# Elementwise work of the mixers taken off GpSimd, the chunk inverse done for two streams at once, and another order of pages and first loads

## The chip, the cores and the metric

The kernel runs on one core of a Trainium2 chip. TensorE (PE) multiplies, VectorE (DVE) and ScalarE (ACT) do elementwise work and read PSUM, GpSimd (POOL) does elementwise work on SBUF, SyncE (SP) issues the DMAs. The metric is the time of one execution on the device in microseconds, as the median of several runs.

## The reference

Two layers over two streams of 256 tokens and 1024 channels, a context `ctx` and the input `x`. In each layer both streams are normalised and modulated by rows computed from `c` (`silu(c) @ w_ada + b_ada`), then pass a mixer, then 16 experts of which each takes its 32 best tokens. The mixer has three branches; the first, gated delta heads, runs in both directions and matters here:

```
q, k = l2_normalize(silu(conv(q))), l2_normalize(silu(conv(k)));  v = silu(conv(v))
decay = exp(gc[i] - gc[j]) for j <= i               # gc: running sum of the gates
m   = strict_lower((k*beta) @ k.T * decay);  a = m + I
u, w = solve(a, v*beta), solve(a, k*beta*exp(gc))   # unit triangular
per chunk:  v_new = u - w @ s
            o     = (q*exp(gc)) @ s + (q @ k.T * decay) @ v_new
            s     = s*exp(g_last) + (k*exp(g_last - gc)).T @ v_new
o = rmsnorm(o_forward + o_backward) * gdn_norm_w * silu(z)
```

The state at the end of `ctx` is the start for `x`. The second branch is a gated token mixing over chunks of 128, the third a pooling; the three are gated, projected and added (`merge`). In layer 1 the context runs only for its states. Experts: `silu(x@w_gate) * (x@w_up) @ w_down`, all in fp32.

## The kernel before

**A recorded program and a planner.** `Net.record` and what it calls write no instructions. Each call on an engine makes an `Op` with its operands (`Prog.record`); `Prog.order` then simulates the engines with a cost for every op (`Prog.cost`), hands out SBUF and PSUM as it goes, and gives each engine a fixed order, which `Prog.emit` issues. An `Eng` with several names (`ad`, `av`, `any`, `vg`) leaves the choice of the engine to the planner. All instructions are issued from one line, so every row of the profile says L623 and tiles are named only `page` (SBUF) and `bank` (PSUM).

**Memory.** SBUF is 25 pages of 2048 fp32 elements per partition. `place` looks for a hole: for short-lived tiles from page 0 up, first in pages of the same size class, then in empty pages, then anywhere; only expert weights take pages in the order in which these became empty. `limits` cap the live tiles of a kind: `wa=5` modulation weights, `w=4` projection weights, `we=18` expert weights. A tile given to a DMA must be free before the DMA can be issued, and SP issues in order.

**PE's two queues.** `order` keeps ready 32x32 matmuls (`op.tile`) apart from the rest, takes them when the wide ones leave room, and leaves a group of them at the latest after twelve (`quad`) if wide ones are ready.

**The order of the work.** `ada_in(0)` loads 16 modulation tiles of 512 KB in two halves, with one pair of matmuls each. `ctx` is loaded ahead of them, `x` after the seventh. Then per layer: norms, `start`, and `gdn`. `gdn` goes over four pairs of heads j. For each it records, for the context and then for `x`, the scan (`heads_scan`) and, behind it, that stream's solve for the next pair (`heads_solve`), and takes pieces of other work (projections, the other branches in `side`) in between, `FILL` many. `pump` mixes in modulation blocks (`ada`), one load step at a time.

**The solve and the inverse.** `heads_solve` builds the decay (`E`, `Eb`), the products with keys and queries (`MT`, `attn`, `qt`) and calls `inverse`: for one stream, 8 matrices of 128x128 (two chunks, two directions, two heads). It inverts the 32x32 diagonal blocks in four levels, each one group of 32 small matmuls, a mask on DVE in two halves, a second group of 32, an add and a transpose; then joins blocks to 64 and to 128 in four more groups. GpSimd does the elementwise steps that carry `G` in the code, and some of those with `vg` and `any`.

**After the heads** come the rest of `side` (gates and branch projections), `merge`, the routing and the experts, whose weights (201 MB a layer) stream in 1 MB tiles.

Of the kernel before, what the change touches and what calls it, by code (L numbers as in the profile page):

```python
# [102 lines left out]
def _layouts(inp):  # L103
# [14 lines left out]
    o["gnw"] = f(g["gdn_norm_w"])  # L118
# [103 lines left out]
class Op:  # L222
    __slots__ = ("i", "eng", "fn", "a", "k", "tiles", "deps", "succ", "nd", "cost", "ready", "start", "end", "on", "prio", "gate", "inst", "win", "tile", "fill")
# [34 lines left out]
class Prog:  # L258
    def __init__(s, nc, pool, banks, limits):
# [6 lines left out]
        s.any = Eng(s, ("act", "dve", "pool"))  # L266
        s.av, s.vg = Eng(s, ("act", "dve")), Eng(s, ("dve", "pool"))
# [13 lines left out]
    def record(s, eng, fn, a, k):  # L281
# [43 lines left out]
        if (not op.deps or eng[0] == "dma") and lim not in ("w", "wa", "we"):  # L325
            op.win = min(op.win, 400)
        if lim in ("w", "wa", "we"):
            op.win = 10 ** 9
        op.tile, op.fill = False, 1.0
# [6 lines left out]
    def cost(s, op, acc):  # L336
# [16 lines left out]
        if op.eng[0] == "pe":  # L353
            if op.fn == "transpose":
                return {"pe": n * 2 / 2.4 + 2}
            m = acc[0][0].shape[0]
            op.fill = min(m, 128) * acc[1][0].shape[0] / 16384
# [3 lines left out]
            c = max(n, m) / 1.2 * 2 + 4  # L361
            return {"pe": c if m > 64 else c * (0.6 if m > 32 else 0.25) + 20 if n < 128 else c * (0.5 if m > 32 else 0.25) + 14}
# [10 lines left out]
    def order(s):  # L373
# [29 lines left out]
        def place(t, spare):  # L403
# [6 lines left out]
            if t.lim == "we":  # L410
                order = sorted(order, key=lambda i: freed[i])
            for step in range(3):
                if step == 1 and sum(g is None for g in pages) <= spare:
                    continue
                for i in order:
                    g = pages[i]
                    if (g is None) != (step == 1) or (g is not None and (g.dt != dt or (step == 0 and g.cls != cls))):
# [39 lines left out]
        def give(t, addr):  # L457
# [9 lines left out]
            if j > 0 and hs[j - 1][1] == a:  # L467
                hs[j - 1:j + 1] = [(hs[j - 1][0], hs[j][1])]
            if hs[0] == (0, PAGE):
                pages[page.i] = None  # L470
                turn[0] += 1
                freed[page.i] = turn[0]
# [11 lines left out]
        recent, group = [], [None, 0]  # L484
# [21 lines left out]
        while left:  # L506
# [6 lines left out]
            while ev and ev[0][0] <= now:  # L513
                _, i, kind = heapq.heappop(ev)
                op = ops[i] if i >= 0 else None
                if kind == 0:
                    for e in op.eng:
                        heapq.heappush(ready["tile" if op.tile else e], (op.prio, op.i))
# [5 lines left out]
            for e in engines:  # L524
# [3 lines left out]
                if e == "pe":  # L528
# [3 lines left out]
                    if ready["tile"]:  # L532
# [5 lines left out]
                        if ready[e] and (x < ready[e][0] and not much or ops[x[1]].a[0].tile is group[0] and group[1] % s.limits["quad"]):  # L538
                            queues.reverse()
                aside, tries = [], 0  # L540
                while queues:
# [26 lines left out]
                    if e == "pe":  # L568
                        if not span[3]:
                            c *= 2  # L570
                        if group[0] is not None and not op.tile:
                            c += 80.0
                        group[1] = group[1] + 1 if op.tile and op.a[0].tile is group[0] else 1
                        group[0] = op.a[0].tile if op.tile else None
                        span[1] += c * op.fill
                        span[2] += c
                        if not op.tile:
# [48 lines left out]
XAT = 6  # L626
# [4 lines left out]
POOLW = (0, 6)  # L631
# [5 lines left out]
FILL = (3, 1, 1)  # L637
ROOM = dict(w=0, wa=0)
EVERY = (0.7, 1.0)
NY = 3  # L640
# [12 lines left out]
class Net:  # L653
# [43 lines left out]
    def run(s):  # L697
        tc, t = s.tc, s.t
        limits = dict(w=4, hi=5, wa=5, we=18, fill=0.94, window=800, spare=0, clock=4096 / 1.2, share=0.5, quad=12, room=ROOM)
# [9 lines left out]
    def record(s):  # L709
# [26 lines left out]
        nc.sync.dma_start(s.xin[0], s.rows[0].rearrange("(t p) d -> p t d", p=128))  # L736
        s.small = {}
        for n, sh in (("n1", [128, 2, 8]), ("conv", [128, 2, 24, 5]), ("psc", [128, 2, 4]), ("wr", [128, 2, 8, 16]),
                      ("alog", [128, 2, 16]), ("dtb", [128, 2, 16]), ("gnw", [128, 2, 128])):
# [8 lines left out]
        for n, _ in enumerate(s.ada_in(0)):  # L748
            if n == EAT:
                s.mark = len(p.ops)  # L750
            if n == XAT:
                nc.sync.dma_start(s.xin[1], s.rows[1].rearrange("(t p) d -> p t d", p=128))
        p.bias = LATE
        nc.sync.dma_start(s.cst[:, C_CUM:C_LEN], t["cst"][:, C_CUM:C_LEN])
        for n in ("conv", "psc", "wr"):
            nc.sync.dma_start(s.small[n], t[n])
        for n, w in (("alog", 16), ("dtb", 16), ("gnw", 128)):
# [59 lines left out]
    def ada(s, l, parts):  # L817

        nc, t = s.nc, s.t
        for g, halves in parts:  # L820
            ps = s.bank("ada")
            js = [j for a in halves for j in (2 * a, 2 * a + 1)]
            for kt in range(8):
                ws = {}
                for a in halves:
# [1021 lines left out]
```

## Time and profile before

| | |
|---|---|
| median of 3 runs | 2430.93 us (2430.82 to 2431.25) |
| profiled execution | 2433.34 us, its span 2431.6 us |
| busy: PE, DVE, ACT, POOL | 2118.4, 1172.9, 647.9, 370.6 us |
| DMA | 603.11 MB, mean 248 GB/s |
| chain that ended last | PE 45%, DMA 36%, DVE 12%, issue 3%, POOL 2%, ACT 1% |

Busy time is the union of an engine's instructions. PEld is the loading of weights, which overlaps PE. A matmul in fp32 shows as two records. The chain of waits is followed back from an end: at each step to what released it; "issue" is time in which nothing that the profile shows was waited for.

### The profile page before, as it was taken

What the parts mean: (1) busy time and instruction counts of PE and PEld (TensorE: products, weight loads), DVE (VectorE), ACT (ScalarE), POOL (GpSimd) and SP (SyncE); (2) the same over time, 40 slices, a digit from 0 to 9 for tenths busy, and PEclk for the clock granted to TensorE, in tenths of its full rate; (3) what the DMA queues carried; (4) which work ended last, traced back from release to release, by engine and by line L of the source; (5) the groups of instructions that cost most, each with busy time, mean ns of one, the idle gap of its engine ahead of it and who ended that gap; (6) DMA issues with size and microseconds to landing.
All of it is one profiled execution on the core that took longest, in us unless ns stands there. A gap on an engine that the chain in (4) does not pass through costs nothing.

```text
span 2431.6 us, 50016 instructions
## 1 busy us (share of the span) xinstructions
PE 2118.4 (87%) x21357; PEld 1351.6 (56%) x21357; DVE 1172.9 (48%) x2712; ACT 647.9 (27%) x1329; POOL 370.6 (15%) x334
## 2 busy tenths in 40 slices
PE   8999999999999999878787899999899977676665
PEld 4777867787779842222222477777789931111211
DVE  4978776854326831212121797788765531010102
ACT  4534343323224520000000454344434420000000
POOL 0233332510000410000000212232330010000000
PEclk9999999999999999999999999999899988888888
DMA  8432333323346689999999634333236879999997
GB/s 291 146 101 82 117 90 99 99 102 101 118 162 203 214 320 421 421 421 421 421 421 421 243 113 152 128 118 122 69 101 217 317 315 421 421 421 421 422 421 307
DMA packets 153910, 603.11 MB, mean 248 GB/s; under 512 B 13820, under 2 KB 60092, under 8 KB 104536
## 3 DMA queue, kind: packets, MB, share of 16 engines
q1 hardware_dynamic: 153688, 599.93, 64.9%
q8 instruction: 167, 2.74, 0.4%
q14 instruction: 55, 0.45, 0.1%
HBM read 597.58 MB, written 2.29 MB: 247 GB/s over the span
## 4 chain that ended last, share of the span: by engine, by line
PE 45%; DMA 36%; DVE 12%; issue 3%; POOL 2%; ACT 1%; SPq 0%; DVEq 0%; ACTq 0%; POOLq 0%
PE bank L623 45%; DMA page<-in_w_up_dram 22%; DVE page L623 12%; DMA page<-in_w_down_dram 12%; POOL page L623 2%; ACT page L623 1%; DMA page<-in_w_gate_dram 0%; DMA page<-in_n_dram 0%; DMA page<-in_b_ada_dram 0%; DMA page<-rows 0%; SPq L623 0%; DMA page<-in_w_ada_dram 0%; DVEq L1843 0%; DVEq L623 0%; POOLq L623 0%
## 5 line engine op out<-in xcount | busy, mean ns | idle before, releaser
L623 PE MATMUL bank<-page,page 32*32 32x32 f32 (+8 forms) x18473 | 2074.4, 335 | 299.6 <-DVE page L623 107.3
L623 PEld LDWEIGHTS bank<-page,page 128*128 128x128 f32 (+5 forms) x18473 | 1300.2, 144 | 1048.4 <-issue 381.3
L623 POOL TENSOR_TENSOR page<-page,page 128x512 f32<-128x512 f32 (+4 forms) x277 | 313.5, 1146 | 1444.1 <-DVE page L623 1050.3
L623 ACT ACTIVATE page<-page 128x1024 fp32r<-128x1024 f32 (+8 forms) x462 | 326.5, 721 | 534.2 <-PE bank L623 273.6
L623 ACT ACTIVATE page<-bank 128x512 f32<-128x512 f32 (+5 forms) x341 | 164.9, 501 | 1106.9 <-PE bank L623 1012.1
L623 DVE TENSOR_TENSOR page<-page,page 128x1024 fp32r<-128x1024 f32 (+6 forms) x389 | 338.5, 888 | 118.9 <-ACT page L623 102.0
L623 DVE TENSOR_TENSOR page<-page,bank 128x256 f32<-128x256 f32 (+2 forms) x184 | 101.4, 558 | 575.9 <-ACT page L623 269.1
L623 DVE TENSOR_TENSOR page<-bank,page 128x128 f32<-128x128 f32 (+4 forms) x350 | 154.5, 460 | 287.2 <-PE bank L623 282.6
L623 ACT ACTIVATE page<-page,page 128x128 f32<-128x128 f32 (+2 forms) x319 | 119.9, 435 | 50.2 <-POOL page L623 31.2
L623 DVE COPY page<-bank 32x128 f32<-32x128 f32 (+7 forms) x175 | 71.4, 408 | 60.9 <-PE bank L623 58.9
L623 DVE SCALAR_TENSOR_TENSOR page<-page,page,page 128x508 f32<-128x508 f32 (+3 forms) x128 | 94.5, 757 | 1.2
L623 DVE SCALAR_TENSOR_TENSOR page<-page,page 128x508 f32<-128x508 f32 (+5 forms) x115 | 75.9, 665 | 14.1 <-DMA page<-in_n_dram 11.7
L623 PE MATMUL bank<-page 32*32 32x32 f32 (+1 forms) x2884 | 76.2, 204 | 2.8 <-DVE page L623 2.4
L623 PEld LDWEIGHTS bank<-page 32*32 32x32 f32 (+1 forms) x2884 | 59.2, 114 | 20.0 <-issue 8.5
L623 POOL MEMSET page<- 128x1024 f32 (+2 forms) x13 | 7.6, 630 | 398.6 <-DMA page<-in_w_up_dram 389.7
L623 DVE TENSOR_SCALAR page<-page 128x4 f32<-128x4 f32 (+7 forms) x215 | 52.6, 258 | 26.2 <-ACT page L623 19.2
L623 DVE STREAM_TRANSPOSE page<-page 32x32 f32<-32x32 f32 (+1 forms) x208 | 57.8, 288 | 4.2
L623 DVE SCALAR_TENSOR_TENSOR page<-page,bank 128x512 f32<-128x512 f32 x48 | 32.7, 684 | 55.9 <-PE bank L623 54.7
L623 ACT ACTIVATE page<-bank,page 128x128 f32<-128x128 f32 (+2 forms) x81 | 36.7, 483 | 78.5 <-PE bank L623 60.0
L623 DVE TENSOR_TENSOR page<-page 128x4 f32<-128x4 f32 (+3 forms) x252 | 50.5, 209 | 4.1
L623 POOL TENSOR_TENSOR page<-page 128x512 f32<-128x512 f32 x22 | 30.9, 1406 | 138.7 <-DVE page L623 96.1
L623 DVE TENSOR_SCALAR page<-page,page 128x128 f32<-128x128 f32 (+3 forms) x125 | 47.4, 416 | 5.2 <-ACT page L623 4.8
(25 smaller groups left out, 235.5 us busy)
## 6 DMA issues: line engine op xcount, KB each, us to landing
page<-in_w_gate_dram SPq DMA_DIRECT2D x128, 1024.0 KB, 19.8
page<-in_w_up_dram SPq DMA_DIRECT2D x128, 1024.0 KB, 19.8
page<-in_w_down_dram SPq DMA_DIRECT2D x128, 1024.0 KB, 19.8
page<-in_w_in_dram SPq DMA_DIRECT2D x136, 512.0 KB, 3.6
page<-in_w_ada_dram SPq DMA_DIRECT2D x96, 512.0 KB, 4.6
page<-rows SPq DMA_DIRECT2D x88, 256.0 KB, 5.0
page<-in_w_br_a_dram SPq DMA_DIRECT2D x24, 512.0 KB, 4.7
page<-in_w_out_dram SPq DMA_DIRECT2D x24, 512.0 KB, 4.6
```

The source lines that it names most:

```text
L623: op.inst = getattr(eng[op.on], fn)(*a, **k)
```

## The change

All elementwise work of the mixers goes to DVE or ACT; GpSimd keeps memsets, the routing's steps and the last norm. `gdn_norm_w` is no longer multiplied into `zs` but is the scale of ACT's last copy (per partition there). The square in `heads_out` becomes four ACT instructions with a running sum, the two products after it one DVE instruction per head and chunk, the state's decay a `scale` on ACT or DVE. `heads_solve` takes both streams, and `inverse` handles 16 matrices in each instruction; `gdn` records it once per j, behind the context's scan. `NY` falls from 3 to 2 buffers, each twice as large. The planner gets other PE costs, puts all matmuls with 64 or fewer rows or columns in the second queue, and stays there while any is ready. Short-lived tiles take pages in the order of their last release, and with more than 8 pages empty also empty ones. The first 16 modulation tiles may all be live (`wi=16`), `ctx` is loaded after the fourth and `x` after the eighth; `ada` loads and multiplies two blocks a step. Core of the diff:

```diff
-            m = acc[0][0].shape[0]
-            op.tile = m <= 32 and acc[1][0].shape[0] <= 32
+            m, k = acc[0][0].shape[0], acc[1][0].shape[0]
+            op.tile = m <= 32 and k <= 32
+            op.part = m <= 64 or k <= 64
             if acc[2][0].dtype == F32R and n >= 256:
-                return {"pe": n / 2.4 + 2}
+                return {"pe": n / 2.4 + 13.5}
...
+            if op.tile:
+                return {"pe": 9.0}
...
-            if t.lim == "we":
+            empty = sum(g is None for g in pages)
+            if not up:
                 order = sorted(order, key=lambda i: freed[i])
-            for step in range(3):
+            for step in range(0 if up or empty <= ROOMY else -1, 3):
...
-    if ready[e] and (x < ready[e][0] and not much or ops[x[1]].a[0].tile is group[0] and group[1] % s.limits["quad"]):
+    if ready[e] and (x < ready[e][0] and not much or group[2]):
         queues.reverse()
...
-XAT = 6
+ROOMY = 8
+XAT = (3, 7)
-POOLW = (0, 6)
-FILL = (3, 1, 1)
+FILL = (6, 1, 2)
-NY = 3
+NY = 2
-        limits = dict(w=4, hi=5, wa=5, we=18, ..., quad=12, room=ROOM)
+        limits = dict(w=4, hi=5, wa=5, wi=16, we=18, ..., room=ROOM)
...
-            if n == XAT:
-                nc.sync.dma_start(s.xin[1], s.rows[1]...)
+            if n in XAT:
+                k = XAT.index(n)
+                nc.sync.dma_start(s.xin[k], s.rows[k]...)
...
-                w = s.p.tile([128, 2, 512], F32, name="wada", lim="wa")
+                w = s.p.tile([128, 2, 512], F32, name="wada", lim="wi" if l == 0 else "wa")
...
-        s.tt(lo, w, hi.bitcast(F32), ALU.subtract, s.p.vg if s.wn > POOLW[s.l] else nc.gpsimd)
+        s.tt(lo, w, hi.bitcast(F32), ALU.subtract)
...
-                if j < 3:
-                    sol[m.k] = s.heads_solve(m, j + 1, qkv[j + 1][m.k], slot(m, j + 1))
+                if j < 3 and m is ms[0]:
+                    sol = s.heads_solve(ms, j + 1, qkv[j + 1], Y[(j + 1) % NY], X[(j + 1) % NY])
                     take(FILL[2])
...
+    def heads_solve(s, ms, j, qkv, Y, XF):
+        MT = [s.p.tile([128, 8, 128], F32, name="MT") for d in range(2)]
+        part = {m.k: s.products(m, j, qkv[m.k], [a[:, 4 * z:4 * z + 4, :] for a in MT]) for z, m in enumerate(ms)}
+        s.inverse(MT, Y, XF)
...
-            s.tt(E, R[0], s.nb[:, :, None, :].to_broadcast(B4), ALU.add, G)
+            s.tt(E, R[0], s.nb[:, :, None, :].to_broadcast(B4), ALU.add)
...
         for lv in range(1, 5):
-            Pn = s.p.tile(C5, F32, name="Pn")
-            for i in range(2):
-                s.tt(Pn[:, i], pp[:, i], s.nm[:, lv, :, None, :].to_broadcast([128, 2, 2, 32]), ALU.mult)
+            Pn = s.p.tile(C4, F32, name="Pn")
+            s.tt(Pn, pp, s.nm[:, lv, :, None, :].to_broadcast(C4), ALU.mult)
```

## Rows read from the trace of the kernel before

**Rows 1.** Stretch, us; busy us (instructions) per engine; PEclk, DMA share, GB/s.

```profile
60.00:520.00 460.00, 434.93 (x7016) 349.27 (x7014) 352.77 (x937) 186.70 (x439) 149.92 (x137) 0.99 0.33 104
520.00:870.00 350.00, 345.93 (x2063) 286.96 (x2061) 175.80 (x272) 122.69 (x191) 44.58 (x31) 1.00 0.48 163
600.00:700.00 100.00, 100.00 (x435) 75.10 (x434) 35.56 (x39) 26.05 (x33) 4.49 (x3) 1.00 0.34 117
950.00:1000.00 50.00, 42.02 (x170) 13.13 (x166) 12.88 (x19) 1.19 (x2) 0.00 (x0) 1.00 1.01 421
1345.00:1820.00 475.00, 439.92 (x7078) 342.88 (x7075) 376.85 (x999) 214.69 (x493) 136.12 (x125) 0.97 0.39 126
128.38:128.95 0.57, 0.57 (x65) 0.57 (x64) 0.57 (x4) 0.57 (x3) 0.00 (x0) 1.00 1.04 423
```

**Rows 2.** Chain of waits, 60 to 520, then 1345 to 1820 us; shares.

```profile
by line: PE bank L623 58.1%; DVE page L623 26.2%; issue 7.8%; POOL page L623 4.7%; ACT page L623 1.6%; DMA page<-rows 1.4%; SPq L623 0.2%; DVEq L623 0.0%; POOLq L623 0.0%; ACTq L623 0.0%
...
by line: PE bank L623 59.8%; DVE page L623 27.7%; issue 6.4%; POOL page L623 3.1%; ACT page L623 3.0%; DVEq L623 0.0%; ACTq L623 0.0%; POOLq L623 0.0%
```

**Rows 3.** PE's weight loads in time order: start, us, form, count, idle before.

```profile
130.12 0.51 PEld L623 LDWEIGHTS bank<-page,page 32*32 32x32 f32 x25 [0.36 <-DVE page L623]
130.87 0.62 PEld L623 LDWEIGHTS bank<-page,page 32*32 32x32 f32 x26 [0.25 <-issue]
131.85 0.22 PEld L623 LDWEIGHTS bank<-page,page 32*32 32x32 f32 x16 [0.36 <-issue]
...
108.19 2.54 PEld L623 LDWEIGHTS bank<-page,page 32*32 32x32 f32 x74 [1.57 <-DVE page L623]
...
516.34 3.62 PEld L623 LDWEIGHTS bank<-page,page 32*32 32x32 f32 x58 [0.32 <-DVE page L623]
...
1435.02 2.14 PEld L623 LDWEIGHTS bank<-page,page 32*32 32x32 f32 x71 [0.37 <-DVE page L623]
...
1797.18 0.80 PEld L623 LDWEIGHTS bank<-page,page 32*32 32x32 f32 x35 [0.33 <-issue]
```

**Rows 4.** Waits in both head stretches: us, times, longest.

```profile
PEld bank L623 <- issue: 33.2, 64, 2.7
...
PEld bank L623 <- issue: 47.0, 97, 3.1
...
DVE page L623 <- ACT page L623: 16.3, 29, 2.0
```

**Rows 5.** DVE by operands, 60 to 520 us: ns min/median/max.

```profile
L623 DVE SCALAR_TENSOR_TENSOR page<-bank,page,page x36: 340/343/351, 203.4 to 475.9; 128x128 f32<-128x128 f32 x36
...
L623 DVE SCALAR_TENSOR_TENSOR page<-page,page,page x60: 704/746/1772, 90.5 to 383.7; 128x508 f32<-128x508 f32 x30, 128x510 f32<-128x510 f32 x30
...
L623 DVE COPY page<-page x48: 172/217/1453, 134.3 to 515.7; 32x128 f32<-32x128 f32 x48
```

**Rows 6.** DVE by form, 60:520, 1345:1820, 1820:1947: busy, mean ns, idle before.

```profile
L623 DVE COPY page<-page 32x128 f32<-32x128 f32 x48 | 13.4, 294 | 0.6
L623 DVE SCALAR_TENSOR_TENSOR page<-page,page,page 128x510 f32<-128x510 f32 x30 | 25.6, 855 | 0.4
L623 DVE STREAM_TRANSPOSE page<-page 128x256 f32<-128x256 f32 x40 | 17.6, 440 | 0.6
L623 DVE TENSOR_TENSOR page<-bank,page 128x128 f32<-128x128 f32 x64 | 15.7, 282 | 17.6 <-PE bank L623 17.6
L623 DVE TENSOR_TENSOR page<-page,bank 128x256 f32<-128x256 f32 x44 | 17.9, 418 | 39.3 <-PE bank L623 39.2
...
L623 DVE COPY page<-page 32x128 f32<-32x128 f32 x58 | 20.6, 376 | 0.6
...
L623 DVE TENSOR_TENSOR page<-page,page 128x512 f32<-128x512 f32 x5 | 3.5, 693 | 0.2
```

**Rows 7.** GpSimd by form, 60 to 520 us: busy, mean ns, idle before.

```profile
L623 POOL TENSOR_TENSOR page<-page,page 128x512 f32<-128x512 f32 x75 | 101.3, 1365 | 230.7 <-DVE page L623 160.3 <-PE bank L623 42.5 <-DMA page<-rows 14.9
```

**Rows 8.** Busy time from 0 to 40 us, columns as in rows 1.

```profile
0.00:40.00 40.00, 29.25 (x127) 11.19 (x129) 13.26 (x43) 14.65 (x23) 4.23 (x11) 0.96 0.88 322
```

More of the change, by code (lines that the diff above doesn't have):

```diff
@@ L222 @@
 class Op:
-    __slots__ = ("i", "eng", "fn", "a", "k", "tiles", "deps", "succ", "nd", "cost", "ready", "start", "end", "on", "prio", "gate", "inst", "win", "tile", "fill")
+    __slots__ = ("i", "eng", "fn", "a", "k", "tiles", "deps", "succ", "nd", "cost", "ready", "start", "end", "on", "prio", "gate", "inst", "win", "tile", "part", "fill")
 class Eng:
@@ L409, in place @@
             order = range(PAGES - 1, -1, -1) if up else range(PAGES)
-            if t.lim == "we":
+            empty = sum(g is None for g in pages)
+            if not up:
                 order = sorted(order, key=lambda i: freed[i])
-            for step in range(3):
-                if step == 1 and sum(g is None for g in pages) <= spare:
+            for step in range(0 if up or empty <= ROOMY else -1, 3):
+                if step == 1 and empty <= spare:
                     continue
@@ L517, in order @@
                     for e in op.eng:
-                        heapq.heappush(ready["tile" if op.tile else e], (op.prio, op.i))
+                        heapq.heappush(ready["tile" if op.part else e], (op.prio, op.i))
                 elif kind == 1:
@@ L570, in order @@
                             c *= 2
[L571 to L574, printed above, removed]
+                        if group[2] and not op.part:
+                            c += 225.0
+                        elif op.part and not group[2]:
+                            c += 95.0
+                        group[2] = op.part
                         span[1] += c * op.fill
                         span[2] += c
-                        if not op.tile:
+                        if not op.part:
                             recent.append((now, c * op.fill))
@@ L1433, in inverse @@
+        yc = s.p.tile([128, 8, 32], F32, name="Y32")
+        V.tensor_copy(yc, yy)
         for a, b in ((0, 1), (2, 3)):
-            V.tensor_copy(Y[Q[a], :, 0, :, 32 * b:32 * b + 32], yy[Q[a]])
-            V.tensor_copy(Y[Q[b], :, 1, :, 32 * a:32 * a + 32], yy[Q[b]])
-        for i in range(2):
-            for h in range(2):
-                V.transpose(XF[Q[1], i, h, 0:32], Y[Q[0], i, 0, h, 32:64])
-                V.transpose(XF[Q[2], i, h, 32:64], Y[Q[3], i, 1, h, 64:96])
+            s.p.av.copy(Y[Q[a], 0, :, 32 * b:32 * b + 32], yc[Q[a]])
+            s.p.av.copy(Y[Q[b], 1, :, 32 * a:32 * a + 32], yc[Q[b]])
```

225 lines of the change are left out of this document (112 added, 113 removed).

## The prediction

> **What bounds the kernel now.** First the stages. The table of busy time by stretch [rows 1] shows two kinds. While a layer's experts run, the DMA share is 1.01 at 421 GB/s and nothing else is full: that part is set by bytes, and the diff changes none of them. In between lie the mixers, about 0 to 880 us and 1345 to 1950 us, at 104 to 163 GB/s. In their second half (520 to 870 in layer 0) PE is busy 99%: a run of 128-wide matmuls with little to gain. In their first half, the delta-rule heads, PE is busy 434.93 of 460 us and 439.92 of 475 us, DVE 77% and 79%, POOL 33% and 29%. A microsecond saved in a mixer moves everything after it, as the expert stream starts when the mixer ends.
>
> Second, the chain of waits over the two head stretches [rows 2]. PE is 58.1% and 59.8% of it, DVE 26.2% and 27.7%, POOL 4.7% and 3.1%, issue 7.8% and 6.4%. So PE is not the bound alone: of 460 + 475 us, DVE holds 120.5 + 131.6 = 252 us and POOL 21.6 + 14.7 = 36 us. Three parts of the change touch these: who does the elementwise work, how many small-matmul groups there are, and how wide the DVE steps between them are.
>
> **Part 1, PE: fewer visits to the small tiles.** The inverse runs 32x32 matmuls; between them PE goes to 128-wide ones. The weight-load rows show what a round trip costs [rows 3]. From 130.12 to 130.87 us are 24 small loads and one wide one (x25): 0.75 us. 64 small matmuls take 0.57 us (128.38 to 128.95) [rows 1], so 24 take 0.21, and a wide one takes 100 us / 435 = 0.23 (600 to 700) [rows 1]. Left: 0.31 us. From 130.87 to 131.85, 24 small and two wide: 0.98 - 0.21 - 0.46 = 0.31 again. It shows as 0.25 to 0.37 us of idle ahead of each group, which the waits call "issue": 33.2 and 47.0 us [rows 4].
> Such groups number 97 in the first head stretch and 89 in the second; [rows 3] shows the first and the last of each. Eight inverses of ten groups would make 80: the old limit of twelve splits some. After, there are four paired inverses of ten groups a layer, and a rule that stays with the partial matmuls while any is ready: 40 + 40. 106 fewer at 0.31 is 33 us; 16 fewer groups of 64-wide matmuls at the same price make 5. PE and issue together hold 66% of the chain, so I take 25 of 38 us (ends 10 and 38).
>
> **Part 2, DVE freed of POOL.** The rows of DVE by operand [rows 5] give minimum, median and maximum. Where an operand lies in PSUM all are alike (340/343/351). Where all lie in SBUF the median is as fast, but the maximum is far off: copies of 32x128 172/217/1453, multiply-adds 704/746/1772. Against means of 294 and 376 ns for those copies and 855 for half of those multiply-adds [rows 6], layer 0 loses 48 x 0.077 + 30 x 0.109 = 7 us, layer 1 58 x 0.159 = 9 us, on forms that hold 39 and 21 us of busy time. Over all forms with SBUF alone I take some 20 us in each, 5.5% of DVE's work [rows 1], an estimate. With no POOL work in the mixers it goes. On the chain: 252 x 5.5% = 14 us (ends 0, and 45 if the blocked instructions all lie on it).
> [...]
>
> **Part 3, POOL's work moved.** What is on POOL's chain now is mostly 128x512 products at 1365 ns [rows 7]; DVE does one in 693 [rows 6]. 36 us on the chain become 18: minus 18 (ends 0, if DVE is queued, and 36). The load on DVE: POOL's 150 + 136 us at half is 143 us more (less, as squares and state scaling go to ACT, 41 to 45% busy, and one product is folded into a copy). Against it stand the 40 us above and the pairing, 74 us. So DVE ends a little above where it is, near 80%.
>
> **Part 4, the paired inverse on DVE.** Rows of the single inverse [rows 6]: a level takes two masks at 0.282, one add at 0.418, one transpose at 0.440, 1.42 us; four levels 5.7. With the nine masks and adds ahead, twelve block copies, eight 32x32 transposes and the last blocks, one inverse takes about 13.4 us by the nearest forms, a pair 26.8. Paired, a level is a mask of 0.69, an add of 0.69 and a transpose of about 0.72 (0.440 and 256 columns more at the 0.0011 by which 0.282 at 128 becomes 0.418 at 256): 2.1; four are 8.4, and the rest, counted in the same way with half the instructions at twice the width, 9.2. That is 17.6, 9.2 us less a pair, 37 a layer. Inverses are 107 of DVE's 353 us, so the chain's share is 252 x 30% x 34% = 26. I take 18, since PE no longer starts on the first half of a mask after 0.282 us but waits 0.69. Ends: 26 gained; 13 lost if all 32 levels wait the 0.4 us unhidden.
>
> **Part 5, the start.** By 40 us 322 GB/s x 40 = 12.9 MB have come, and PE is busy only 29 of the 40 us [rows 8]. Of the sixteen modulation tiles only five may live, so a load waits for the matmuls of one five ahead, and SP's queue with it. At 421 GB/s the bytes take 30.6 us. With 16 tiles nothing holds back the issues; ctx and x lie behind four and eight of them. At most 9 us; PE already has wide matmuls in between from 32 us, so I take 6 (ends 0 and 9).
>
> **Part 6, what I put at nothing.** Taking pages in the order of release removes waits on pages just let go; the nearest row is DVE's waits for ACT, 16.3 us in 29 [rows 4], few of which can be that: 0, up to 10 gained. It may cost room: Y and X64 grow from 3 x 1280 to 2 x 2560 elements, MT and one more set of attn and qt add some 3,000, two or three of 25 pages. Three megabytes of expert weights less fetched ahead are 7.5 us at 421 GB/s a layer: 0 to 15 lost. I take 0 because these tiles are dead when the experts are fetched. Two modulation blocks a step under the limit of five tiles have less lead, but PE goes to them half as often; no wait for them stands among PE's long ones, so 0, to 2 lost.
>
> **Sum.** 25 + 14 + 18 + 18 + 6 = 81. Span 2431.6 - 81 = 2350.6; the profiled execution took 2433.3, 1.7 more than its span and 2.4 more than the median, so 2350 against 2430.93. Its own range: 2305 to 2400.
>
> **Rivals.**
> *Only the visits pay* (0.18). DVE and POOL work is hidden behind PE, and the chain goes back to PE when they shrink. For it: PE is busy 93 to 95% of the head stretches. Against: 252 us of DVE on the chain. 25 + 6 = 31 saved: 2400.
> *DVE takes it back* (0.07). The 143 us land on a DVE that is already busy 77 and 79% [rows 1] and the savings of part 4 do not come on the chain. 143 - 74 - 45 = 24 more, which eats the visits: 2430.
> *One long chain* (0.16, slower). Paired, the solve is a single chain of 12 PE and DVE steps on which both streams' scans of the next head pair wait, where two inverses used to cover each other. Its length: a level is two PE rounds of about 1.45 us (DVE waits 39.2/44 = 0.9 now, for half the matmuls [rows 6]) and 2.1 of DVE, 5.0; four are 20; start 4.8 and the last blocks 8: 33 us, eight times 264. It decides when more than 81/8 = 10 us of each finds no wide matmul to cover it; at 13 us uncovered, 104 - 81 = 23 is lost: 2455. For it: layer 1 has fewer queries to project and already more PE idle, 35 against 25 us. Against: 97 groups a layer wait now, and the wide matmuls that cover them are not fewer.
> [...]
>
> **Chances.** Forecast 0.59, rivals 0.18, 0.07, 0.16. Under 0.2% (5 us) I cannot tell a change: faster 0.77, same 0.07, slower 0.16. The range to 2436 takes in all but the slower rival; 2300 leaves out the ends where all parts pay in full.
>
> **What would show it.** Right: about 40 small-tile groups a layer; copies of 32 rows near their median of 217, no maximum over 1 us; POOL empty between 90 and 870 us; DVE's share of the chain under 24%; the first modulation's bytes in by 32 us; expert streams of the same length, each starting earlier by the mixer's gain (45 in layer 0, 36 in layer 1). Wrong: PE idle above 25 and 35 us in the head stretches with DVE named, DVE over 85%, or a first expert stream that starts no earlier.

## The result and the profile after

The changed kernel takes 2406.24 us (2403.55 to 2411.24, 4 runs) against 2431.07 on the same chip: ratio 0.99 (95% 0.9881 to 0.992), 25 us less. 81 were forecast, to 2350, in a range of 2305 to 2400. The profiled execution took 2403.55 us, its span 2401.8.

First the busy time by stretch of the changed kernel; columns as in [rows 1].

```profile
60.00:520.00 460.00, 416.18 (x7072) 345.63 (x7072) 337.02 (x821) 199.84 (x489) 0.00 (x0) 0.96 0.34 104
520.00:870.00 350.00, 342.18 (x2031) 287.23 (x2030) 177.96 (x308) 129.09 (x219) 19.61 (x12) 0.99 0.49 169
1345.00:1820.00 475.00, 424.79 (x7281) 361.04 (x7282) 360.96 (x877) 248.16 (x576) 0.00 (x0) 0.95 0.40 132
0.00:40.00 40.00, 30.92 (x134) 11.27 (x135) 15.83 (x46) 14.56 (x23) 5.26 (x9) 0.91 0.94 355
```

GpSimd is empty in both head stretches, DVE does less than before (337 for 353, 361 for 377) although it took over GpSimd's work, and the first 40 us bring 355 GB/s for 322 [rows 8]. All that was meant. But PE is less busy too: 43.8 us idle of 460 where 25.1 were, 50.2 of 475 where 35.1 were, and its clock is granted at 0.96 and 0.95 instead of 0.99 and 0.97. PE has fewer microseconds to do and waits more.

The chain of waits, first and second head stretch, to be held against [rows 2]:

```profile
by line: PE bank L629 59.2%; DVE page L629 23.7%; issue 7.4%; ACT page L629 4.8%; DMA page<-rows 2.8%; ACT L629 1.1%; DMA page<-in_w_ada_dram 0.9%; SPq L629 0.2%; DVEq L629 0.0%; ACTq L629 0.0%
...
by line: PE bank L629 73.9%; DVE page L629 10.9%; issue 8.7%; ACT page L629 4.5%; DMA page<-in_w_ada_dram 1.2%; ACT L629 0.8%; SPq L629 0.1%; ACTq L629 0.0%; DVEq L629 0.0%
```

GpSimd has left it, and DVE's share fell. "issue" hardly moved, although the forecast took it for the mark of the visits, and these fell: counted as changes from any other matmul to a 32x32 one, from 126 and 125 in the two stretches to 40 and 39. The waits say where it sits now (both stretches, us, times, longest; compare [rows 4]):

```profile
PEld bank L629 <- issue: 48.0, 72, 2.8
DVE page L629 <- ACT page L629: 34.9, 34, 5.4
PE bank L629 <- issue: 22.3, 21, 2.7
...
PEld bank L629 <- issue: 54.6, 74, 2.6
PE bank L629 <- issue: 32.2, 30, 2.4
```

There are fewer idle times at "issue" than there were visits before, but those of the weight loads (PEld) are longer: 0.67 and 0.74 us on the mean, where [rows 4] gives 0.52 and 0.48. Many lie inside the groups. These are weight loads in order of time, the levels of one paired inverse (columns as in [rows 3]):

```profile
1719.85 2.57 PEld L629 LDWEIGHTS bank<-page,page 32*32 32x32 f32 x127 [0.71 <-issue]
1723.69 2.40 PEld L629 LDWEIGHTS bank<-page,page 32*32 32x32 f32 x128 [1.27 <-issue]
1727.44 2.39 PEld L629 LDWEIGHTS bank<-page,page 32*32 32x32 f32 x128 [1.34 <-issue]
1730.91 2.55 PEld L629 LDWEIGHTS bank<-page,page 32*32 32x32 f32 x128 [1.08 <-issue]
1734.65 2.78 PEld L629 LDWEIGHTS bank<-page,page 32*32 32x32 f32 x128 [1.19 <-issue]
```

Each piece ends after 127 or 128 loads, which with their 128 matmuls are 256 instructions; then PE stands for about a microsecond, and the next piece begins 3.5 to 3.8 us after the last began. No engine is named. The time of the first whole piece by engine, columns as in [rows 1]:

```profile
1719.85:1723.69 3.84, 2.69 (x128) 2.40 (x127) 0.69 (x1) 0.00 (x0) 0.00 (x0) 1.00 0.02 4
```

DVE is busy 0.69 us, ACT and GpSimd not at all, the clock is full, and the DMA engines are almost idle. What has 256 instructions is a packet of the program itself, in the list of DMA queues (packets, MB, share of 16 engines):

```profile
q8 instruction: 167, 2.74, 0.5%
```

2.74 MB in 167 packets are 16.4 KB each; PE's 2 x 21,357 instructions in 167 parts are 256. Two runs below show the same: e1 has 16,384 more of PE's instructions, 8192 matmul records each with its load, and 64 packets more (231); e5 has 8192 fewer and 32 packets fewer (135); 256 to a packet each time. The packets' own times in the trace tie the pauses to them. One packet is under way from 1721.09 to 1722.29, and the piece at 1723.69 begins 1.40 us after its end; the next starts 1.30 us into that piece, at 1724.99, ends at 1726.06, and the piece at 1727.44 begins 1.38 us after that. Of the 33 pauses over 0.8 us between two small matmuls in the changed kernel, 31 end 1.2 to 1.75 us after the end of a packet. So the 3.5 to 3.8 us are about 1.1 to 1.3 until the next packet starts, 0.9 to 1.2 for the packet, and 1.4 to 1.6 until PE goes on.

A run of small matmuls is through a packet's 256 instructions before the next is there: the supply is the slower side, 3.5 to 3.8 us for what PE loads in 2.4 to 2.8. Wide matmuls are not: a record of one takes 0.23 us [rows 1] for two instructions, its load and its matmul, so 256 last some 29 us by estimate. From 600 to 700 us of the changed kernel packets start at 622.73, 647.54 and 678.85, and PE is busy all of the 100 us. This, then, is the first suspect.

The second is the chain. Three stretches of ten microseconds at two places, columns as in [rows 1]:

```profile
420.00:430.00 10.00, 4.82 (x21) 4.38 (x22) 9.46 (x20) 1.06 (x1) 0.00 (x0) 0.70 0.34 105
1695.00:1705.00 10.00, 1.88 (x15) 1.49 (x13) 9.51 (x22) 9.97 (x31) 0.00 (x0) 0.78 0.18 55
1705.00:1715.00 10.00, 6.88 (x166) 6.20 (x170) 6.46 (x13) 1.08 (x3) 0.00 (x0) 0.50 0.01 3
```

And PE's timeline at the second place, the end of the context's scan and the start of the paired inverse:

```profile
1696.16 1.38 PE L629 MATMUL bank<-page,page 128*128 128x128 f32 x10 [0.66 <-DVE page L629]
1705.70 0.58 PE L629 MATMUL bank<-page,page 128*128 128x128 f32 x1 [8.16 <-DVE page L629]
```

From 1697.5 to 1705.7 PE has nothing: DVE makes the products of both streams and the paired inverse's masks, ACT is full as well, and PE's order, which the planner has fixed, puts no matmul beside them. From 1705 to 1715 the clock is at 0.50. Ten-microsecond stretches of the heads in which PE is busy under 7 us number 3 before and 8 after; with the single inverse put back (run e4, below) there are none.

To hold the runs against each other, the time of PE in the mixers (start to the routing of layer 0, and the same of layer 1) is split by the records of the trace. Each interval from one matmul's start to the next holds the matmul's own time by form (0.23 us for 512 columns, 0.0087 for a small one), 0.31 for a visit, and the rest. The rest is "cold" up to the nominal time where the clock was low; "supply" where it exceeds 0.3 us and ends 0.9 to 1.75 us after the end of an instruction packet (by chance that would take up at most a tenth: 167 windows of 0.85 us in 1500); otherwise, over 0.3, "wait". us:

| | time | visits | supply | wait | cold |
|---|---|---|---|---|---|
| before | 2431 | 100 | 26 | 102 | 18 |
| changed | 2406 | 37 | 68 | 112 | 27 |
| e1 matmuls doubled | 2659 | 38 | 160 | 118 | 87 |
| e2 share 0.85 | 2373 | 33 | 38 | 116 | 25 |
| e4 single inverse | 2380 | 65 | 39 | 92 | 15 |
| e5 matmuls halved | 2311 | 38 | 5 | 113 | 12 |
| e6 single, share 0.85 | 2359 | 63 | 24 | 83 | 11 |
| e7 GpSimd's work moved, nothing else | 2389 | 100 | 11 | 87 | 10 |
| e8 PE's queue and costs, nothing else | 2438 | 63 | 37 | 138 | 29 |

So by this account the visits paid 63 us where 38 were put at most, but supply took back 42, waits 10 and the clock 9. The four columns are not all of the difference: they leave out the matmuls' own time and what is under 0.3 us. What of a gap is a visit and what a wait is a convention, as 0.31 us is set for each visit; supply does not hang on it. Two rows are of executions faster than the median in the column "time": e6 2346.78, e7 2382.83 us.

### The profile page after: what moved, and what is told of

It reads as the page before. It is cut to its first block, busy times and chain, and to the rows that moved or that the text cites. A ratio compares the mean times of both kernels' runs of the same rounds, so it can differ in the third digit from the quotient of the medians.

```text
span 2401.8 us, 49340 instructions
## 1 busy us (share of the span) xinstructions
PE 2047.9 (85%) x21357; PEld 1338.4 (56%) x21357; DVE 1128.9 (47%) x2476; ACT 683.4 (28%) x1466; POOL 49.0 (2%) x41
## 3 DMA queue, kind: packets, MB, share of 16 engines
q8 instruction: 167, 2.74, 0.5%
## 4 chain that ended last, share of the span: by engine, by line
PE 46%; DMA 38%; DVE 9%; issue 4%; ACT 3%; SPq 0%; DVEq 0%; ACTq 0%
PE bank L629 46%; DMA page<-in_w_up_dram 16%; DMA page<-in_w_down_dram 12%; DVE page L629 9%; DMA page<-in_w_gate_dram 7%; ACT page L629 2%; DMA page<-in_w_ada_dram 1%; DMA page<-in_w_in_dram 1%; DMA page<-rows 1%; DMA page<-in_b_ada_dram 0%; ACT L629 0%; DMA page<-in_n_dram 0%; SPq L629 0%; DVEq L1851 0%; DVEq L629 0%
## 5 line engine op out<-in xcount | busy, mean ns | idle before, releaser
L629 PE MATMUL bank<-page,page 32*32 32x32 f32 (+11 forms) x20144 | 2022.0, 324 | 337.6 <-DVE page L629 112.1
L629 PEld LDWEIGHTS bank<-page,page 32*32 32x32 f32 (+7 forms) x20144 | 1308.3, 143 | 1041.1 <-issue 385.7
L629 ACT ACTIVATE page<-page 128x1024 fp32r<-128x1024 f32 (+7 forms) x487 | 341.1, 719 | 495.5 <-PE bank L629 250.3
L629 DVE TENSOR_TENSOR page<-page,page 128x1024 fp32r<-128x1024 f32 (+3 forms) x470 | 403.3, 882 | 149.2 <-ACT page L629 122.7
L629 DVE TENSOR_TENSOR page<-page,bank 128x512 f32<-128x512 f32 (+2 forms) x152 | 97.1, 645 | 578.2 <-ACT page L629 261.6
L629 DVE TENSOR_TENSOR page<-bank,page 128x256 f32<-128x256 f32 (+4 forms) x286 | 148.0, 531 | 280.3 <-PE bank L629 270.8
L629 DVE SCALAR_TENSOR_TENSOR page<-page,page,page 128x508 f32<-128x508 f32 (+4 forms) x176 | 100.8, 594 | 1.5 <-ACT page L629 0.3
L629 DVE COPY page<-bank 128x512 f32<-128x512 f32 (+7 forms) x103 | 54.4, 529 | 52.6 <-PE bank L629 51.0
L629 DVE SCALAR_TENSOR_TENSOR page<-page,page 128x512 f32<-128x512 f32 (+5 forms) x104 | 72.9, 710 | 12.2 <-DMA page<-in_n_dram 7.8
L629 POOL TENSOR_TENSOR page<-page,page 128x512 fp32r<-128x512 f32 (+1 forms) x16 | 20.7, 1321 | 1916.6 <-ACT page L629 1467.6
L629 DVE TENSOR_SCALAR page<-bank,page 128x128 f32<-128x128 f32 (+3 forms) x54 | 27.7, 522 | 63.1 <-PE bank L629 54.6
L629 DVE TENSOR_SCALAR page<-page,page 128x128 f32<-128x128 f32 (+2 forms) x136 | 41.3, 340 | 1.0 <-ACT page L629 0.4
```

Of the source, the lines that this page charges most:

```text
L629: op.inst = getattr(eng[op.on], fn)(*a, **k)
```

## The experiments

Two theories. A: the paired groups outrun their instructions. B: supply is beside the point, and the chain through DVE, made single by the pairing, sets the time. All ratios are against the kernel before on the same chip. Its median there lies between 2431.07 and 2436.38 us, so a difference of times between two runs is good to some 5 us; gains are also given against each run's own before.

**e1**, the changed kernel; each 32x32 matmul of the levels issued twice.

```diff
-                    s.mm(pp[Q[q], d, u, :], MT[d]..., X[Q[q], d, u, :], True, True)
+                    for _ in range(2):
+                        s.mm(pp[Q[q], d, u, :], MT[d]..., X[Q[q], d, u, :], True, True)
...
```

> Changed kernel, but every 32x32 matmul of the four levels is issued twice into the same place (same result). Theory A, instruction supply: PE's instructions come in packets of 16 KB, and a group of 64 small matmuls is one packet by itself, so a doubled group is two. Where little wide work stands between the groups each of the 64 level groups then pays one more wait of 1.2 to 3.7 us inside the group: 80 to 220 us more, 2485 to 2625, with idle inside small-tile groups and no engine named for it. Theory B, the chain between PE and DVE: only PE's own 0.56 us per group is added, 64 x 0.56 = 36 us at most and partly hidden: 2405 to 2440.

Measured 2659.46, ratio 1.0941 (1.0913 to 1.0969), worse even than A. The queue of instructions and PE's small matmuls in it (form, count, busy, mean ns, idle before and by whom):

```profile
q8 instruction: 231, 3.78, 0.6%
```

```profile
L629 PE MATMUL bank<-page,page 32*32 32x32 f32 x15520 | 209.9, 212 | 132.8 <-issue 124.8 <-DVE page L629 7.9
L629 PE MATMUL bank<-page 32*32 32x32 f32 x1888 | 27.4, 216 | 18.1 <-issue 18.1
```

64 packets more cost 253 us. The matmuls' own time is 8192 records at 0.57 us per 64 [rows 1], 73. Of the other 180 the account gives 92 to supply and 60 to the clock, which is granted at 0.87 and 0.90 in the two head stretches for 0.96 and 0.95, while PE stands idle 68.6 and 83.5 us there for 43.8 and 50.2.

**e5**, the opposite: one weight serves two neighbouring units, so half the instructions. The weights of every second unit are left out; the steps on DVE stay.

```diff
-            for (d, u) in units:
+            for (d, u) in units[::2]:
...
-                    s.mm(pp[Q[q], d, u, :], MT[d]..., X[Q[q], d, u, :], True, True)
+                    s.mm(pp[Q[q], d, u:u + 2, :], MT[d]..., X[Q[q], d, u:u + 2, :], True, True)
...
```

> Changed kernel with half the instructions in the four levels: each 32x32 weight is applied to two neighbouring units (64 columns), and the odd units' own weights are left out, so the inverse is not computed. DVE's rounds, widths and the order of the work stay. Theory A, instruction supply: a group is half a packet, idle inside groups in both layers falls from 68 us to 35 or less, and with it the slow-clock time: 2350 to 2380. Theory B, the chain: PE's part of a round shrinks by at most 0.5 us and the waits stay: 2395 to 2406.

Measured 2310.95, ratio 0.9499 (0.9475 to 0.9524), under A's range too. Supply is gone (5 us), with the same visits and the same waits. Of the 95 us less than the changed kernel 63 are supply, 15 clock, and some 17 the matmuls' own time: 4096 records of 64 columns follow each other at 14.8 ns in their runs, where 8192 of 32 columns did at 9.5. So the run does not give supply's price alone, but by the account nothing is left for the chain. B's bounds are out in both runs.

**e2**, the changed kernel; the planner prefers wide matmuls to ready small ones for longer.

```diff
-        limits = dict(..., clock=4096 / 1.2, share=0.5, room=ROOM)
+        limits = dict(..., clock=4096 / 1.2, share=0.85, room=ROOM)
```

> Changed kernel, but the planner asks for more wide matmuls before it goes to a small-tile group (share 0.85 in place of 0.5). Theory A: groups lie further apart, a packet lasts longer, idle inside groups falls from 55 us in both head stretches to under 35, time 2385 to 2400. Theory B: the rounds of the inverse come later, waits for DVE rise by 10 to 30 us, time 2410 to 2430.

Measured 2372.81 (0.9738 to 0.9778), under A's range and far from B's: 33 us less than the changed kernel (36 against its own before), of which supply gives 30, with no change of the work.

**e3**, the same kernel, leave a run of partial matmuls after 16.

```diff
-    if ready[e] and (x < ready[e][0] and not much or group[2]):
+    if ready[e] and (x < ready[e][0] and not much or group[2] and group[1] % 16):
```

> Changed kernel, but the planner may leave a run of partial matmuls after 16. Theory A: wide matmuls inside a group slow the demand for instructions, so idle inside groups falls under 25 us; but groups of small tiles rise from about 40 to 100 or more a layer at 0.31 us each, 35 us more in both: time 2400 to 2425. Theory B: nothing is gained inside the groups and the visits are paid: 2425 to 2445.

Measured 2394.63 (0.9819 to 0.9852), under both ranges. The visits stayed nearly as they were (43 and 43 in the head stretches for 40 and 39) and supply was 73: the rule did not split the groups, so this says nothing of A or B. It shows that another order of the same work can be worth 10 us and more.

**e4**, the changed kernel with the single inverse of before, one stream at a time.

```diff
-NY = 2
+NY = 3
-FILL = (6, 1, 2)
+FILL = (3, 1, 1)
...
-    def heads_solve(s, ms, j, qkv, Y, XF):
+    def heads_solve(s, m, j, qkv, slot):
...
-        C4 = [128, 2, 8, 32]
+        C5 = [128, 2, 2, 2, 32]
```

> Changed kernel, but with the inverse of one stream at a time as before (groups of 32, three buffers, FILL 3,1,1), on DVE and ACT only. Theory A: a group is half a packet, idle inside groups falls by 25 to 35 us, 80 more visits cost 25: time 2395 to 2415, no clear difference. Theory B (one long chain): with two chains that cover each other the waits for DVE and ACT fall by 20 us or more against the changed kernel; time 2375 to 2395. Forecast's part 4 (DVE relief by pairing is worth 18): 2425.

Measured 2379.51 (0.9757 to 0.9789), in B's range: pairing, with the buffers and the `FILL` that come with it, costs 27 us, or 30 with each against its own before. What it does to the small matmuls, by where their operands lie, here in e4 and then in the changed kernel:

```profile
L629 PE MATMUL bank<-page,page 32*32 32x32 f32 x6656 | 85.5, 195 | 14.0 <-issue 10.3 <-DVE page L629 3.4
L629 PE MATMUL bank<-page 32*32 32x32 f32 x2560 | 33.9, 198 | 15.4 <-issue 15.2
```

```profile
L629 PE MATMUL bank<-page,page 32*32 32x32 f32 x8192 | 98.3, 199 | 41.0 <-issue 38.8 <-DVE page L629 2.1
L629 PE MATMUL bank<-page 32*32 32x32 f32 x1024 | 13.0, 204 | 4.9 <-issue 4.8
```

The same 9216 records have 29.4 us of idle before them in e4 and 45.9 in the changed kernel. In the account pairing saves 28 us of visits and pays 29 for supply, 20 for waits and 11 for the clock: A and B are both true of it.

**e6**, e4 and e2 in one.

> The single inverse of the last call and the wider spacing (share 0.85) together. Theory A: what both remove is partly the same, 39 us left with the single inverse fall to 25: 2360 to 2372. Theory B: spacing delays the chain's rounds, waits rise by 10 or more and undo it: 2378 to 2395.

Measured 2358.7 (2346.78 to 2362.56; 0.9683 to 0.973), just under A's range, with the lowest waits of all.

**e7**, the kernel before; all that GpSimd does in the mixers goes to DVE or, where the planner may choose, ACT.

```diff
-        s.any = Eng(s, ("act", "dve", "pool"))
-        s.av, s.vg = Eng(s, ("act", "dve")), Eng(s, ("dve", "pool"))
+        s.any = Eng(s, ("act", "dve"))
+        s.av, s.vg = Eng(s, ("act", "dve")), Eng(s, ("dve",))
...
-            s.tt(E, R[0], s.nb[...].to_broadcast(B4), ALU.add, G)
+            s.tt(E, R[0], s.nb[...].to_broadcast(B4), ALU.add)
...
```

> Kernel before with only GpSimd's elementwise work of the mixers on DVE, same forms, old inverse, old planner. By the forecast's parts 2 and 3 (14 and 18 us on the chain): 2395 to 2405. If DVE's time is hidden behind PE: 2425 to 2435, with DVE 5 to 10 points busier and its waits unchanged.

Measured 2389.1 (0.9808 to 0.9858), under both ranges: this part alone, with the old forms of the steps, is worth 42 us, 17 more than the whole change. Its chain in the two head stretches, and DVE in the first by operands (ns min/median/max; [rows 5]):

```profile
by line: PE bank L623 89.3%; DVE page L623 6.6%; DMA page<-rows 2.4%; issue 1.1%; ACT page L623 0.4%; SPq L623 0.2%; DVEq L623 0.0%; ACTq L623 0.0%
...
by line: PE bank L623 72.6%; DVE page L623 20.7%; issue 3.4%; ACT page L623 1.7%; DMA page<-rows 1.4%; SPq L623 0.2%; DVEq L623 0.0%; ACTq L623 0.0%
```

```profile
L623 DVE COPY page<-page x57: 171/217/225, 128.5 to 498.6; 32x128 f32<-32x128 f32 x57
L623 DVE SCALAR_TENSOR_TENSOR page<-page,page,page x48: 707/742/750, 95.1 to 366.8; 128x508 f32<-128x508 f32 x24, 128x510 f32<-128x510 f32 x24
```

PE's waits for DVE in both stretches (us, times, longest), in the kernel before and then in e7:

```profile
PEld bank L623 <- DVE page L623: 32.0, 47, 2.9
PE bank L623 <- DVE page L623: 15.4, 18, 2.7
...
PEld bank L623 <- DVE page L623: 39.3, 55, 4.0
PE bank L623 <- DVE page L623: 23.6, 22, 3.1
```

```profile
PEld bank L623 <- DVE page L623: 13.1, 31, 0.8
PE bank L623 <- DVE page L623: 0.8, 3, 0.5
...
PEld bank L623 <- DVE page L623: 20.7, 43, 2.4
PE bank L623 <- DVE page L623: 6.0, 10, 2.2
```

These waits fall from 110 us to 41, and DVE's part of the chain from 26.2% to 6.6% and from 27.7% to 20.7%, although DVE has 38 and 19 us more work in the two stretches (391 for 353, 396 for 377). So its load is not what held PE up. The maxima of 1453 and 1772 ns are gone. Over all DVE instructions with operands in SBUF alone, the time above the median of their form was 29 and 34 us in the two stretches before, lost by 76 instructions of over 0.3 us each; in e7 and in the changed kernel there is none. Where an operand lies in PSUM there was none before either. The same edit takes GpSimd's own slow steps off the chain (1365 ns for what DVE does in 693, [rows 7] and [rows 6]); what share of the 42 us is theirs and what share the late results', no run tells apart.

**e8**, the kernel before with the new PE costs and the queue of partial matmuls alone.

```diff
+            op.part = m <= 64 or k <= 64
...
-                        if ready[e] and (x < ready[e][0] and not much or ops[x[1]].a[0].tile is group[0] and group[1] % s.limits["quad"]):
+                        if ready[e] and (x < ready[e][0] and not much or group[2]):
```

> Kernel before with only the planner's new PE costs and its queue of partial matmuls. By the price of 0.31 us a visit and 60 to 80 visits fewer: 19 to 25 us saved, less 5 to 15 us more idle inside groups (theory A): 2410 to 2425. If visits are hidden behind the chain: 2428 to 2434.

Measured 2437.93 (1.0008 to 1.0048), above both ranges. 37 us of visits are saved and nothing comes of it: waits rise by 36, supply and the clock's cost by 11 each. With GpSimd still in the chain PE waits for DVE 87.7 us in the second head stretch, where it waited 62.9.

**e9**, the kernel before with the new first loads alone; **e10**, the changed kernel with the old choice of pages.

```diff
-XAT = 6
+XAT = (3, 7)
...
-        limits = dict(w=4, hi=5, wa=5, we=18, ...
+        limits = dict(w=4, hi=5, wa=5, wi=16, we=18, ...
...
```

> The kernel before with part 5 alone: the 16 first modulation tiles may all live, ctx is loaded after the fourth, x after the eighth. Forecast's part 5: 6 us less, ratio 0.9965 to 0.9985. Rival, the start is hidden behind the first projections or given back before the experts: 0.999 to 1.001. Theory A (instruction supply) has no say here, since no matmul is added, removed or moved between queues.

```diff
-            if not up:
+            if t.lim == "we":
                 order = sorted(order, key=lambda i: freed[i])
-            for step in range(0 if up or empty <= ROOMY else -1, 3):
+            for step in range(3):
```

> The changed kernel with the old choice of pages (part 6 undone). Forecast's part 6, nothing: within 5 us of the changed kernel, 2401 to 2411. Rival, taking pages in the order of release removed waits that now come back: 2415 to 2430. Other rival, the new choice spreads tiles and holds up expert weights: 2380 to 2398, with a layer's expert stream 5 us shorter or its start earlier.

e9 took 2443.25 (1.0028 to 1.0064), slower by 11; e10 2395.72 (0.9838 to 0.9864), 10 less than the changed kernel. The DMA view of e9, 0 to 60 us:

```profile
DMA packets 5683, 16.22 MB, mean 270 GB/s; under 512 B 1236, under 2 KB 2004, under 8 KB 5681
```

That is 270 GB/s where the same view has 291 before, 318 after and 299 in e10. Sixteen live tiles by themselves make the start slower; with the rest of the change and the old pages they make it faster than before, and the new pages add to that. What else in the change the start needs was not tried. For the rest of the kernel the new pages show no gain. e10's time lies in the range of the rival by which they hold up expert weights, but the sign of that is missing: layer 0's first expert load is issued at 822.6 us in e10, later than the 812.5 of the changed kernel.

**e11, e17**, the kernel before with e7's edit, the share at 0.75 and the first loads of e9; and with e7's edit and the share at 0.85 alone.

> The kernel before with three things: GpSimd's work on DVE (as e7), the new first loads, and the planner's share at 0.75 instead of 0.5, so that wide matmuls are preferred to small groups for longer. Theory A (the share pays because groups of small matmuls outrun their instruction packets): e7 has little such idle time, 11 us, so the share brings at most 5 and the start 6: 2376 to 2386. Theory B (the share pays because wide matmuls are kept for the time in which the chain of the inverse runs): as in e2 and e6, 20 to 30 us on top of the start: 2350 to 2366.

> e7 (the kernel before with GpSimd's work on DVE, 2389.1) with the share at 0.85 and the first loads as before. If the first loads, put on the old choice of pages, cost e11 its gain: 2365 to 2392 here. If the share did, which in a planner with the old matmul prices keeps small groups back that the scans need: 2420 to 2445. Theory A (instruction supply) foresees no gain from the share here, since e7 has 11 us of such idle time.

2442.22 (1.0026 to 1.0056) and 2549.52 (1.0443 to 1.0487). Both expectations of e11 fell, and e17, slower than either of its ranges, costs 160 us over e7: waits go from 87 to 198. The share that helps under the new matmul prices and queue ruins the old planner. That it was the share is shown in e17, which has nothing else over e7; why the old planner takes it so is not.

**e12, e18**: e6 with the share at 0.95, and e6 with the old pages.

> The changed kernel with the single inverse of before and the share at 0.95 (e6 had 0.85 and 2358.7). Theory A: another 24 us of idle time inside groups is left in e6, of which a part goes: 2345 to 2358. Theory B (held back too long, the small groups make the scans late and PE waits for DVE): 2362 to 2380.

> The changed kernel with the single inverse, the share at 0.85 and the old choice of pages: e6 (2358.7) and e10 (10.5 us less than the changed kernel) in one. If e10's gain is the pages': 2342 to 2353. If it was the order's scatter of some 5 to 10 us: 2353 to 2370.

2356.83 (0.968 to 0.9716) and 2359.19 (0.9643 to 0.9698), both the same as e6 within their intervals. Supply falls to 12 in e12 while waits rise to 115: the two are traded. e10's gain does not come again, as scatter of the order would have it; that the old pages pay only beside the paired inverse is not excluded. e6, e12 and e18 are the fastest kernels with all of the work, some 48 us under the changed one.

**e13 to e16**, how much of a verdict is the planner's luck: its estimate of the delay behind a matmul moved by 2 ns of 60, to 62, and to 58 in the changed kernel.

```diff
-        limits = dict(..., spare=0, clock=4096 / 1.2, share=0.5, ...)
+        limits = dict(..., spare=0, slack=62.0, clock=4096 / 1.2, share=0.5, ...)
```

> The kernel before, the planner's estimate of the delay behind a matmul 2 ns longer (62 for 60), which is no change of the work and only reshuffles the order. If the planner's orders scatter little: within 5 us of the kernel before. If they scatter by the 10 us and more that e3, e8 to e10 suggest: anywhere from 2420 to 2445.

> e7 (the kernel before with GpSimd's work on DVE, 2389.1) with the same nudge of 2 ns. If e7's gain of 42 us comes from taking GpSimd out: 2380 to 2405. If it was a lucky order, as the loss of e11 lets one think: 2410 to 2440.

> e4 (the changed kernel with the single inverse, 2379.5) with the same nudge. If pairing costs some 25 us whatever the order: 2370 to 2392. If e4 was luck: 2395 to 2415, no better than the changed kernel.

> The changed kernel (2406.24), its planner's delay 2 ns shorter (58 for 60; at 62 the planner finds no order). If pairing costs 25 us whatever the order: 2396 to 2416. If the changed kernel's order was bad luck: 2370 to 2392, as good as the single inverse.

Measured: before 2426.76 (0.9934 to 0.9982), e7 2382.07 (0.9772 to 0.9804), e4 2375.18 (0.9732 to 0.9774), changed 2407.71 (0.9873 to 0.9908). Against its own before none moves by more than 9 us. GpSimd's part (51 us here) and pairing's cost (33 here) are no luck as far as one other order each can tell; the 10 to 15 us of e3, e9 and e10 are of the size of such scatter or little above it.

## Why the prediction was wrong

The term that failed is part 4, the paired inverse: 18 us were put as gained, and with its visits it cost 30. Part 1's 25 us came to nothing by themselves, and parts 2 and 3 brought more than their 32. Each gain against the kernel before on its own chip, in us:

| from before to changed | forecast | runs | with the nudge |
|---|---|---|---|
| GpSimd's work (parts 2, 3): e7 | 32 | 42 | 51 |
| queue, start, pages and reshaped steps, without pairing: e4 less e7 | 31 less pairing's visits | 12 | 7 |
| pairing (part 4 and its visits): changed less e4 | 18 and its visits | -30 | -33 |
| sum (of unrounded gains) | 81 | 25 | 26 |

*Part 4, the paired inverse, failed in its sign.* "I take 18" rested on DVE's shorter bill, and that came as worked out: masks 686 ns, adds 684, transposes 706, 2.08 us a level for 2.1; DVE's busy time fell. But the gain was put on the chain in proportion to DVE's share of it, and the cost side was bounded by 0.4 us a level. Two things were not in the bounds. Groups of 64 matmuls wait for their instructions, 42 us over the mixers more than before and 29 more than with the single inverse. And the products and masks of both streams now stand in one block between a scan and its inverse, 8.16 us of PE idle at 1697, with the clock at 0.50 after it (1705 to 1715). In e4, with the DVE steps of the pair broken up again, 20 us of waits go by the account, more than the bound of 13, and PE's waits for DVE fall from 85 to 50 us in the head stretches. The 29 us of supply stood in no bound of the prediction.

*Part 1, the visits: the new count right, their worth wrong.* There are 40 + 39 groups for the 40 + 40 foreseen. Before there were 126 + 125 by the records, not 97 + 89, so more went than was forecast, and the account, at the forecast's price, saves 63 us of visits for the 38 put as the upper end. Yet by themselves they give nothing (e8), since PE then waits for DVE, and behind e7 they turn into supply, 11 to 39 from e7 to e4. The 0.66 by which PE and issue stood in the chain was no share of what comes through. "issue" in [rows 4] was read as the price of a visit, but the account finds 26 us of supply already in the kernel before.

*Parts 2 and 3: right, and too low.* 42 to 51 for 32. That the late DVE instructions come from GpSimd's work, on which the 14 us of part 2 rest, was the author's assumption, as no row of the kernel before shows it; e7 does, with copies of at most 225 ns for 1453. The estimate took 20 us of DVE's time as lost so in each head stretch; it was 29 and 34. e7 shows the chain through DVE nearly dissolved in the first stretch and shorter in the second. The 143 us that DVE would take over did not hurt: 38 and 19 us more busy in e7, as the late time went and ACT took its part.

*Part 5: 6 foreseen.* The first store of the mixer's rows came 7.3 us earlier, 72.5 for 79.8, so at that place the 6 are there. But the new first loads by themselves (e9) put it at 82.1 and the whole kernel 11 us later; with all but the new pages (e10) it is at 75.6. Some 3 us of the gain are thus of part 6, which was put at nothing.

*The milestones.* The first expert load of layer 0 is issued at 812.5 for 828.7, and the last of the `w_gate` loads of layer 1 at 2352.7 for 2381.0: 16 and 28 us, where 45 and 81 were foreseen. Of the 16 only 8 are left when layer 0's routing ends (its last index matmul starts at 872.8 for 881.2); there the changed kernel has, columns as in [rows 1]:

```profile
800.00:820.00 20.00, 17.42 (x153) 16.78 (x153) 19.86 (x37) 8.21 (x11) 4.63 (x3) 1.00 0.51 182
820.00:850.00 30.00, 29.61 (x194) 27.36 (x194) 16.02 (x24) 10.89 (x26) 6.73 (x4) 0.89 0.63 235
850.00:880.00 30.00, 22.74 (x121) 10.56 (x122) 13.65 (x47) 8.99 (x22) 9.84 (x8) 0.83 0.81 297
```

DVE is full for 20 us, PE idles, and the clock is at 0.89 and 0.83. Which edit does this was not tried. When the last expert load of layer 0 is issued, 7 us are left (1321.7 for 1328.3), so layer 0 gives 7 of the 45 foreseen and layer 1 22 of 36. Pairing's cost, too, sits in layer 0: in e4 that load is issued at 1302.0, 20 us before the changed kernel, and the last one of layer 1 24 us before it (2341.5 for 2365.1), so layer 1 adds only 4. With the nudges (e16 less e15) layer 0 has 31 and layer 1 has 2. Why layer 1 bears the pairing almost without loss, although the wait of 8.16 us above is there, stays open.

*The signs.* Of the prediction's signs of being wrong one came in part: PE idle 43.8 and 50.2 us in the head stretches, above 25 and 35, though with "issue" named more than DVE.

*The rivals.* "DVE takes it back" is out: DVE is less busy. "Only the visits pay" (2400) comes near the time by luck: by themselves the visits pay nothing, and GpSimd's part pays most. "One long chain" named one half of the mechanism, the waits, with its sign for pairing right, but not the supply, and not the size for the whole change.

## What to carry to other kernels

Here a stall that no engine explained, after every 127 or 128 weight loads, was the program's own supply: 31 of 33 pauses end 1.2 to 1.75 us after a packet. At such a stall look at the packets of the instruction queue before fusing small matmuls into longer runs, and try wide matmuls between them: by the account e2 brought supply from 68 to 38 us that way. Fewer visits, or fewer and larger instructions, pay only if what is saved lies on the chain, and a share of the chain is no factor by which a saving comes through: the new queue alone gave nothing, and pairing cost 30 us. When a planner sets the order, run each edit alone, and once more with a nudge that does not change the work, before trusting differences of ten microseconds.

## What the runs showed of the hardware

- PE's instructions come in packets of 16.4 KB, 256 instructions (167 packets for 42,714; 231 and 135 in e1 and e5); a run of small fp32 matmuls takes one each 3.5 to 3.8 us though its weight loads in that time last 2.4 to 2.8 us (1719.85 to 1737.43). PE goes on 1.4 to 1.6 us after a packet's end, and the next packet starts 1.0 us or more after that. Twice the matmuls cost 253 us, of which 73 are their own.
- GpSimd's work made single DVE instructions on SBUF late: copies of at most 225 ns without it (e7) had gone to 1453 with it, and 63 us were lost so in the two head stretches, none where an operand lay in PSUM. Moving the work to DVE and ACT gained 42 to 51 us in all, although DVE then had 38 us more to do in the first head stretch.
